# Moving attention's output ahead of DeltaNet's chain in a hybrid decoder trunk

## The chip, the core and the metric

The kernel runs on one core of a Trainium2 chip. The metric is the device time of one execution in microseconds (us), the median over runs. The engines are TensorE (PE, matrix products), VectorE (DVE), ScalarE (ACT, table functions and copies), GpSimd (POOL) and SyncE (SP, which issues the loads). Each takes its own instructions strictly in the order in which they stand, and waits at one until the data or the buffer that it needs is there.

## The reference

A trunk of two layers over 272 tokens (16 learned ones and 256) of width 1024. Each layer is

```
h = h + 0.5 * swiglu(rmsnorm(h))          # ffn1
h = h + mixer(rmsnorm(h))
h = h + 0.5 * swiglu(rmsnorm(h))          # ffn2
```

The mixer projects once to the inputs of three groups of heads and joins their outputs:

```
sb_q, sb_k, sb_v, dn_qkv, dn_z, dn_b, dn_a, s5_u = split(h @ w_in)
o_sb = rmsnorm(stick_breaking_attention(q, k, v))
qkv  = silu(causal_conv(dn_qkv))                     # q, k, v: 2 blocks of 128 columns each
o_dn = rmsnorm(chunk_gated_delta_rule(l2norm(q), l2norm(k), v, g, beta)) * silu(dn_z)
y    = gelu(s5_states_out);  o_s5 = rmsnorm(y * sigmoid(y @ w_glu + b))
return concat(o_sb, o_dn, o_s5) @ w_out
```

In the delta rule v enters only as `v * beta`. silu(x) is x·sigmoid(x), which equals 0.5·x·(tanh(x/2)+1).

## The kernel before, in words

Activations are held transposed, 128 features by 272 tokens a block. Every projection is made of three products for each pair of blocks (`mm3`, lines 139 to 143): high part by high part (L141), the activations' low part (L142), the weights' low part (L143). The weights come by DMA in pieces of 128x1024; ACT rounds a piece to its high part (`wh`, L133), and DVE or POOL subtracts to get the low part (`wl`, L136). A piece has 24 products, so a "unit" of one 128-column block is 24 products.

`mixer` works through a list of steps by hand, `MIX`. Its letters: `C0` to `C5` are the projections and causal convolutions of DeltaNet's q, k, v (two blocks each), `Q K V Z` other projections, `U`, `p`, `t`, `y` the S5 group's inputs, projections, states and outputs (`y`: products `pY`, then GELU on ACT), `g` the gates, `i` one step of the inversion of DeltaNet's triangular matrices (products `px` and `py` with copies by ACT and DVE between them), `a` one step of attention (scores, weights, and last two outputs, one for each half), `l` the silu of DeltaNet's q and v, `v` the transposed values of attention (`pvs`), `r` one step of DeltaNet's chain over its chunks, `x` one step of the S5 group's gate (`pglu`), `n` the switch of ACT's table back to Ln and Exp, `m` the S5 group's norm, `S` the part of the output projection that needs the S5 group alone, `o` DeltaNet's norm and output. The parts of the output projection that need all groups (`Y`) come after the list. The list only sets in which order the code emits its steps; a scheduler then fixes the order within each engine, and it may move an instruction past others that don't depend on it.

Attention's output step (L1271 to 1287) is, for each half: six products `pob`, a square by ACT, two products `pnb`, then Ln and Exp on ACT, three Newton steps on DVE (L118 to 120), the scaling of the output (L1284), and the split into a high part `xh` (ACT) and a low part `xl` (DVE), where the output projection reads it.

PSUM has four tags of two buffers each: `a` (projections, gate, half of the output projection), `b` (S5 and parts of DeltaNet), `c` (attention), `d` (inversion, `pob`). The scratch tile `cv` has three buffers that the convolution's `pad`, attention's `sbr` and `sby`, `zt` and others share in turn. ACT holds one set of functions at a time: Ln with Exp, silu, or GELU with tanh. `phase` loads another, and the loads keep their place among the functions that need them.

## Time and profile before

| quantity | value |
|---|---|
| runs | 1170.92, 1174.08, 1177.52 us; median 1174.08 |
| the profiled execution | 1172.99 us, its span 1170.9 us |
| TensorE | 97% of the span busy, mean granted clock 0.983 |
| VectorE, ScalarE, GpSimd | 73%, 53%, 17% |
| projections and the two ffn downs (L141 to L143) | 6 groups of products, 1840 or 528 instructions each |

The mixer of the first layer lies at about 230 to 406 us of the span, that of the second at 811 to 984. In the view of windows a PEclk of 1.00 is 2.4 GHz and 0.50 is 1.2 GHz; a window between them holds both levels. In the waits, `A <- B` means that A stood still until B was done.

### The profile page before, as it was taken

Reading aid. Unit: us, or ns where it says so; the run is one execution under the profiler, and the core shown is the slowest. Engines: PE = TensorE matmul, PEld = TensorE weight load, DVE = VectorE, ACT = ScalarE, POOL = GpSimd, SP = SyncE. Lnnn points to the kernel's source line nnn. Section 1 sums busy time; section 2 is a strip of 40 time slices with the busy share of each in tenths; the row PEclk is TensorE's granted clock in tenths of the full one; section 3 lists DMA queues with packets and bytes.
Section 4 is the critical chain, followed back from the end, with each engine's and each line's share of the span. In section 5 each row is a group of like instructions: output and inputs, shape, how many; then the busy total and the mean of one; then the engine's idle time right before and its main releaser. Section 6 shows DMA issues by size and latency. Waiting matters only on the chain.

```text
span 1170.9 us, 23748 instructions
## 1 busy us (share of the span) xinstructions
PE 1140.0 (97%) x9544; PEld 1091.7 (93%) x9544; DVE 858.5 (73%) x1609; ACT 620.5 (53%) x993; POOL 194.0 (17%) x242
## 2 busy tenths in 40 slices
PE   8999999999998999999999999999999989999997
PEld 7999999998896999999999999999988969999985
DVE  7999986599656965565569998756995678666544
ACT  6455465464663654444454555645545737545533
POOL 6312101113310111110202111011141001111100
PEclk9999999999998999999999999999999979999998
DMA  5655544542221455555565565455332216556663
GB/s 186 183 174 174 169 149 151 166 127 60 87 73 55 146 172 173 176 180 163 184 180 168 167 193 163 137 179 156 107 91 74 85 43 198 181 181 189 191 196 109
DMA packets 196858, 173.74 MB, mean 148 GB/s; under 512 B 21300, under 2 KB 193004, under 8 KB 196748
## 3 DMA queue, kind: packets, MB, share of 16 engines
q1 hardware_dynamic: 196732, 172.22, 48.6%
q8 instruction: 75, 1.23, 0.4%
q14 instruction: 35, 0.29, 0.1%
q10 hardware_dynamic: 16, 0.00, 0.0%
HBM read 171.15 MB, written 1.05 MB: 147 GB/s over the span
## 4 chain that ended last, share of the span: by engine, by line
PE 83%; DVE 10%; POOL 2%; ACT 2%; issue 2%; DMA 1%; SPq 0%; ACTq 0%; DVEq 0%; POOLq 0%
PE proj L143 17%; PE proj L142 17%; PE proj L141 17%; PE pd L143 5%; PE pd L142 5%; PE pd L141 5%; PE pd L490 5%; DVE wl L136 2%; PE pY L847 1%; POOL TT L1010 1%; PE pm L780 1%; POOL t L1009 1%; PE pob L1275 1%; PE pY L845 1%; DVE s5z L836 1%
## 5 line engine op out<-in xcount | busy, mean ns | idle before, releaser
L141 PE MATMUL proj<-xh,wh 128*128 128x272 f32 (+1 forms) x1840 | 524.8, 291 | 1.5 <-DVE sy L1424 1.5
L142 PE MATMUL proj<-xl,wh 128*128 128x272 f32 (+1 forms) x1840 | 521.9, 290 | 0.3 <-DVE xl L1222 0.3
L143 PE MATMUL proj<-xh,wl 128*128 128x272 f32 (+1 forms) x1840 | 493.4, 291 | 1.5 <-DVE wl L136 1.2
L133 ACT ACTIVATE wh<-raw 128x1024 fp32r<-128x1024 f32 (+1 forms) x324 | 338.2, 1044 | 291.5 <-PE proj L142 102.2
L136 DVE TENSOR_TENSOR wl<-raw,wh 128x1024 fp32r<-128x1024 f32 (+1 forms) x312 | 378.7, 1214 | 146.2 <-PE pd L143 60.5
L141 PEld LDWEIGHTS proj<-xh,wh 128*128 128x128 f32 x1840 | 348.8, 190 | 4.3 <-DVE sy L1424 2.6
L142 PEld LDWEIGHTS proj<-xl,wh 128*128 128x128 f32 x1840 | 348.3, 189 | 2.4 <-DVE xl L1222 0.5
L143 PEld LDWEIGHTS proj<-xh,wl 128*128 128x128 f32 x1840 | 331.4, 189 | 3.9 <-DVE wl L136 2.9
L432 POOL TENSOR_TENSOR hl<-h,hh 128x272 fp32r<-128x272 f32 (+1 forms) x88 | 80.8, 921 | 452.4 <-ACT hh L431 451.5
L141 PE MATMUL pd<-hh,wh 128*128 128x272 f32 x528 | 149.8, 289 | 0.0
L142 PE MATMUL pd<-hl,wh 128*128 128x272 f32 x528 | 149.5, 288 | 0.0
L143 PE MATMUL pd<-hh,wl 128*128 128x272 f32 x528 | 141.1, 289 | 0.2
L141 PEld LDWEIGHTS pd<-hh,wh 128*128 128x128 f32 x528 | 99.3, 188 | 0.2
L142 PEld LDWEIGHTS pd<-hl,wh 128*128 128x128 f32 x528 | 99.4, 188 | 0.1
L143 PEld LDWEIGHTS pd<-hh,wl 128*128 128x128 f32 x528 | 95.2, 189 | 1.0 <-DVE wl L136 0.9
L104 ACT ACTIVATE g<-g 128x272 f32<-128x272 f32 (+2 forms) x92 | 37.7, 415 | 68.8 <-DVE g L426 68.7
L431 ACT ACTIVATE hh<-h 128x272 fp32r<-128x272 f32 (+1 forms) x88 | 36.3, 419 | 50.7 <-DVE h L430 50.6
L430 DVE TENSOR_TENSOR h<-proj,g 128x272 f32<-128x272 f32 (+1 forms) x88 | 37.8, 434 | 32.3 <-PE proj L143 20.6
L426 DVE TENSOR_TENSOR g<-proj,R 128x272 f32<-128x272 f32 (+1 forms) x88 | 37.5, 431 | 18.3 <-PE proj L143 18.1
L428 DVE TENSOR_TENSOR g<-g,R 128x272 f32<-128x272 f32 (+1 forms) x88 | 37.8, 434 | 12.5 <-ACT g L104 12.2
L136 POOL TENSOR_TENSOR wl<-raw,wh 128x1024 fp32r<-128x1024 f32 x12 | 29.4, 2452 | 97.0 <-PE proj L143 31.9
L373 POOL TENSOR_TENSOR acc<-acc,sq 128x272 f32<-128x272 f32 (+1 forms) x20 | 23.1, 1153 | 91.9 <-ACT sq L367 91.3
(490 smaller groups left out, 1295.4 us busy)
## 6 DMA issues: line engine op xcount, KB each, us to landing
raw<-in_ffn_w_gate_dram SPq DMA_DIRECT2D x88, 512.0 KB, 3.6
raw<-in_ffn_w_up_dram SPq DMA_DIRECT2D x88, 512.0 KB, 3.7
raw<-in_ffn_w_down_dram SPq DMA_DIRECT2D x70, 512.0 KB, 3.5
raw<-in_w_in_dram SPq DMA_DIRECT2D x36, 512.0 KB, 4.3
raw<-in_ffn_w_down_dram SPq DMA_DIRECT2D x24, 384.0 KB, 3.0
raw<-in_w_out_dram SPq DMA_DIRECT2D x16, 512.0 KB, 3.4
raw<-in_s_w_glu_dram SPq DMA_DIRECT2D x4, 512.0 KB, 4.7
xin<-in_x_dram SPq DMA_DIRECT2D x4, 256.0 KB, 6.1
```

The costliest lines, as they stand in the source:

```text
L104: i = self.nc.scalar.activation(out, in_, func, **k)
L133: nc.scalar.activation(h[:, :n], r[:, :n], AF.Copy)
L136: e.tensor_tensor(l[:, :n], r[:, :n], f32(h[:, :n]), op=ALU.subtract)
L141: mm(p, wh, xh, start=first, stop=False)
L142: mm(p, wh, xl, start=False, stop=False)
L143: mm(p, wl, xh, start=False, stop=last)
L426: V.tensor_tensor(g1, pg[j][:, :N], R, op=ALU.mult)
L428: V.tensor_tensor(g1, g1, R, op=ALU.mult)
L430: V.tensor_tensor(h, pu[j][:, :N], g1, op=ALU.mult)
L431: nc.scalar.activation(hh[:, f, :N], h, AF.Copy)
L432: G.tensor_tensor(hl[:, f, :N], h, f32(hh[:, f, :N]), op=ALU.subtract)
L490: PE.matmul(pd[i][e], x[:, f, ts], w[:, 0, e * 512:e * 512 + 512], start=f == 0 and w is h and x is hh, stop=f == NF - 1 and w is lo)
```

## The change

The list is written anew. Attention's two output steps leave the end (they stood as `a` among the last `r` steps) and come before the table switch `l`; their result is written into q's place in SBUF (`q[:, b, :]`) instead of a scratch buffer, and a new step `w` (`sb_split`) makes its high and low part later, behind the second `x`. The transposed values `v` come before that, and so do `V0`, `V1`. The projections of DeltaNet's v, `C4` and `C5`, move from before `l` to behind `y0` and `y1`. Their silu no longer is among those of `l` but is made of a tanh: `twice_silu` gives (tanh(x/2)+1)·x, twice the silu, as `do_z` already did, and the half is put into beta (`beh`, one new small DVE instruction in `dn_gates`), which multiplies v later. `ON_POOL` names by their number the pieces whose low part POOL makes; the numbers stay, the pieces behind them change with the list.

```diff
@@ -39,8 +39,8 @@
-MIX = "C2 C3 U0 g U1 g g U2 g g g U3 g Q0 p0 p1 Q1 t0 p2 p3 K0 i t1 K1 a a t2 C0 a a i C1 i t3 a a i C4 i a a i C5 l i " \
-      "y0 V0 i y1 V1 i y2 Z0 y3 Z1 v r r r r x r r x r n a r r r r a m S4 S6 o S0 S2"
+MIX = "C2 C3 U0 g U1 g g U2 g g g U3 g i Q0 p0 p1 Q1 t0 p2 p3 K0 i t1 K1 i a a t2 V0 a i a C0 i a a t3 V1 i a a v i C1 a i a l " \
+      "r y0 C4 r i y1 C5 y2 r Z0 y3 r Z1 r x r x w r r n r r r m S4 S6 o S0 S2"
 ON_POOL = (5, 7, 10, 15, 20, 25)
 NBUF = (3, 2, 3)
 LO_POOL = 5
@@ -909,7 +909,9 @@
         V.tensor_copy(bet[:, 8:9], pg[:, 16:17])
         V.tensor_tensor(b8(x), pgv[:, :, 1, :], b8(dtb), op=ALU.add)
         V.tensor_tensor(x[:, 8:9], pg[:, 17:18], dtb[:, 8:9], op=ALU.add)
-        self.bet = bet
+
+        self.beh = tl([P, 9], "beh")
+        V.tensor_scalar(self.beh, bet, 0.5, None, op0=ALU.mult)
         yield
         self.phase(SET_LNEXP)
         V.scalar_tensor_tensor(g, x, -1.0, x, op0=ALU.mult, op1=ALU.min)
@@ -1087,7 +1089,7 @@
         V, G, A, PE = nc.vector, nc.gpsimd, nc.scalar, nc.tensor
         psum = lambda nm: self.psum("d", nm)
         tl, hsl, kn, TTf = self.dn_tile, self.hsl, self.kn, self.TTf
-        bet, eg, egl, el, beg = self.bet, self.eg, self.egl, self.el, self.beg
+        beh, eg, egl, el, beg = self.beh, self.eg, self.egl, self.el, self.beg
         quad = [slice(32 * q, 32 * q + 32) for q in range(4)]
         unit = lambda c, h: 4 * (h % 2) + 2 * c + h // 2
@@ -1115,7 +1117,7 @@
                 PE.transpose(pv[:, 256 + b * P:256 + b * P + P], kn[:, b, c * P:c * P + P], self.ident)
             v, k = tl([P, 4, 64], "vb", 2), tl([P, 4, 64], "kg", 2)
             pvv = pv.rearrange("p (h d) -> p h d", d=64)
-            V.tensor_tensor(v, pvv[:, 0:4], bc(bet[:, 4 * c:4 * c + 4], 2, 64), op=ALU.mult)
+            V.tensor_tensor(v, pvv[:, 0:4], bc(beh[:, 4 * c:4 * c + 4], 2, 64), op=ALU.mult)
             V.tensor_tensor(k, pvv[:, 4:8], bc(egl[:, 4 * c:4 * c + 4], 2, 64), op=ALU.mult)
             vb.append(v)
             kg.append(k)
@@ -1123,7 +1125,7 @@
         for h in range(4):
             PE.matmul(pv[32 * h:32 * h + 32, 0:64], qkv[hsl(h), 4 + h // 2, 256:288], self.ident[hsl(h), hsl(h)], start=True, stop=True)
         vbt = tl([P, 64], "vbt")
-        V.tensor_scalar(vbt, pv[:, 0:64], bet[:, 8:9], None, op0=ALU.mult)
+        V.tensor_scalar(vbt, pv[:, 0:64], beh[:, 8:9], None, op0=ALU.mult)
         yield
         qf = qkv.rearrange("p b t -> p (b t)")
@@ -1275,17 +1277,21 @@
                 PE.matmul(p[:, 0:272], vt[0][:, h, :], W[h][:, 0:272], start=True, stop=False)
                 PE.matmul(p[:, 128:272], vt[1][:, h, :], W[h][:, 272:416], start=False, stop=False)
                 PE.matmul(p[:, 256:272], vt[2][:16, h, :], W[h][:16, 416:432], start=False, stop=True)
-            r, y = self.cv("sbr")[:, :T], self.cv("sby")[:, :T]
+            r, y = self.cv("sbr")[:, :T], q[:, b, :]
             A.activation(r, po[:, :T], AF.Square)
             pn = psum("pnb")
             PE.matmul(pn[:, :T], self.bd64, r, start=True, stop=True)
             self.rsqrt(r, pn[:, :T], scale=1.0 / 64, bias=self.eps)
             self.newton(r, pn[:, :T], y, 64, EPS)
             V.scalar_tensor_tensor(y, po[:, :T], self.sbg[:, l], r, op0=ALU.mult, op1=ALU.mult)
-            h = self.xh[:, slot + b, :]
-            A.activation(h, y, AF.Copy)
-            V.tensor_tensor(self.xl[:, slot + b, :], y, f32(h), op=ALU.subtract)
-
+
+        def split():
+            for b in range(2):
+                h = self.xh[:, slot + b, :]
+                A.activation(h, q[:, b, :], AF.Copy)
+                V.tensor_tensor(self.xl[:, slot + b, :], q[:, b, :], f32(h), op=ALU.subtract)
+
+        self.sb_split = split
         for f, x in ((scores, 0), (scores, 1), (weights, 0), (scores, 2), (weights, 1), (scores, 3),
                      (weights, 2), (weights, 3), (outputs, 0), (outputs, 1)):
             f(x)
@@ -1357,6 +1363,12 @@
             ba = tmp.tile([8, TP], F32, name="ba")
             G.memset(ba[:, T:], 0.0)
+            def twice_silu(x):
+
+                t = self.cv("ts")[:, :T]
+                self.act(t, x, AF.Tanh, scale=0.5)
+                V.scalar_tensor_tensor(x, t, 1.0, x, op0=ALU.add, op1=ALU.mult)
+
             def conv(b):
                 src = w_in[:, 768 + b * P:768 + b * P + P]
                 if b == 2:
@@ -1372,6 +1384,8 @@
                     V.scalar_tensor_tensor(y, pad[:, k:k + T], self.cw[:, l, k, b:b + 1], y, op0=ALU.mult, op1=ALU.add)
                 if b in (2, 3):
                     self.act(y, y, AF.Silu)
+                elif b > 3:
+                    twice_silu(y)
             u = tmp.tile([P, 4, T], F32, name="s5u")
             zr = tmp.tile([P, 2, T], F32, name="pz")
@@ -1387,16 +1401,12 @@
                 V.scalar_tensor_tensor(dst[:, b, :], p[:, :T], 0.125 if c0 == 0 else 1.0, R, op0=ALU.mult, op1=ALU.mult)
             def do_z(b):
-
                 proj(1536, zr, b)
-                t = self.cv("zt")[:, :T]
-                self.act(t, zr[:, b, :], AF.Tanh, scale=0.5)
-                V.scalar_tensor_tensor(zr[:, b, :], t, 1.0, zr[:, b, :], op0=ALU.add, op1=ALU.mult)
+                twice_silu(zr[:, b, :])
             def silu():
                 self.phase(SET_SILU)
-                for b in (0, 4):
-                    self.act(qkv[:, b:b + 2, :T], qkv[:, b:b + 2, :T], AF.Silu)
+                self.act(qkv[:, 0:2, :T], qkv[:, 0:2, :T], AF.Silu)
                 self.phase(SET_GELU)
             def norms():
@@ -1429,7 +1439,7 @@
                           a=self.sb(l, q, k, v, 0), x=self.glu(l, u))
             steps = dict(C=conv, U=s5_in, Q=lambda b: proj(0, q, b), K=lambda b: proj(256, k, b), V=lambda b: proj(512, v, b),
                          Z=do_z, p=lambda r: self.s5_inputs(u, r), t=self.s5_states, y=lambda r: self.s5_outputs(u, r),
-                         l=silu, v=lambda: self.sb_values(), n=norms, S=lambda d0: w_out_part("S", d0, "ab"[d0 // 2 % 2]),
+                         l=silu, v=lambda: self.sb_values(), w=lambda: self.sb_split(), n=norms, S=lambda d0: w_out_part("S", d0, "ab"[d0 // 2 % 2]),
                          o=lambda: (self.dn_norm(), self.dn_out(zr, self.dng[:, l], 2)),
                          m=lambda: self.rms(self.acc, 4 * 512, 0, self.R5, "b"))
             for x in MIX.split():
```

Three places show what the order within the engines becomes.

TensorE, from the inversion's third product (`px`, L1040 before and L1042 after) on. Before:

```order
L141 MATMUL proj<-xh,wh 128x272
L1040 MATMUL px_4060<-T_4047,LT 32x32 x16
L142 MATMUL proj<-xl,wh 128x272
...
L143 MATMUL proj<-xh,wl 128x272
L845 MATMUL pY<-s5U,M_591 128x68
L847 MATMUL pY<-s5z_3458,W_589 128x68
...
L1053 MATMUL py_4127<-kb,TT_4048 32x32 x8
L1056 MATMUL py_4127<-TT_4048,kb 32x32 x16
L847 MATMUL pY<-s5z_3458,W_590 128x68
```

After:

```order
L143 MATMUL proj<-xh,wl 128x272
L1042 MATMUL px_4042<-T_3975,LT 32x32 x16
L1055 MATMUL py_4087<-kb,TT_3976 32x32 x8
L1058 MATMUL py_4087<-TT_3976,kb 32x32 x16
L1277 MATMUL pob<-W_587 64x272
...
L1075 MATMUL px_4181<-T_3975,LT 64x32 x8
L1277 MATMUL pob<-W_587 64x272
...
L1080 MATMUL py_4302<-TTf,X_4170 64x64 x8
L1283 MATMUL pnb<-sbr,bd_385 128x272
L141 MATMUL proj<-xh,wh 128x272
```

Fourteen projection products and five of S5's outputs stood between `px` and `py`; none does now. The inversion's and attention's small products stand in one row, and the projection behind the second `pnb` is Z's first.

VectorE, around the convolution of C4 and the decays `E` of DeltaNet. Before, where `E` is made:

```order
L1318 SCALAR_TENSOR_TENSOR s5u_3079<-th_4466,s5u_3079 128x272
L1324 SCALAR_TENSOR_TENSOR xl_95<-s5u_3079,prm_361,xh_94 128x272 x3
L883 TENSOR_TENSOR E_3299<-pl_4422,E_3299 128x512
L1330 TENSOR_TENSOR rs_4467<-rs_4467,gsq_4586 128x272
L887 TENSOR_TENSOR Et_3359<-plt_4428,Et_3359 128x32
```

After, from attention's second output on:

```order
L1286 SCALAR_TENSOR_TENSOR pq_3081<-pob_4191,prm_361,sbr_4198 128x272
L1381 TENSOR_TENSOR pad_4274<-proj_4243,R_3061 128x272
L1384 SCALAR_TENSOR_TENSOR qkv_3075<-pad_4274,prm_361,qkv_3075 128x272 x3
L1370 SCALAR_TENSOR_TENSOR qkv_3075<-ts_4281,qkv_3075 128x272
L1381 TENSOR_TENSOR pad_4361<-proj_4330,R_3061 128x272
L1384 SCALAR_TENSOR_TENSOR qkv_3075<-pad_4361,prm_361,qkv_3075 128x272 x3
L1105 TENSOR_SCALAR eq_4224<-pn_4211 128x9
...
L1370 SCALAR_TENSOR_TENSOR pz_3080<-ts_4445,pz_3080 128x272
L1292 TENSOR_TENSOR xl_95<-pq_3081,xh_94 128x272 x2
L883 TENSOR_TENSOR E_3301<-pl_4290,E_3301 128x512
L887 TENSOR_TENSOR Et_3361<-plt_4296,Et_3361 128x32
```

`pq` is q's place. C4's `pad`, which empties the PSUM buffer that Z's first projection writes, stands behind attention's second output; `eq` stands behind C5's convolution, and the second `E` behind the two splits of attention's output.

TensorE at the end of DeltaNet's chain. Before:

```order
L1161 MATMUL pS<-qkv,E 128x64 x4
L1281 MATMUL pnb<-sbr,bd_385 128x272
L1176 MATMUL pkt<-qkv,kn 32x64
...
L1177 MATMUL pkt<-qkv 32x64
L1184 MATMUL pvt_4646<-rt_4642,TTt 32x64 x4
L1188 MATMUL pvt_4646<-vnt,Et 32x64 x4
L1275 MATMUL pob<-W_587 64x272
```

After:

```order
L1179 MATMUL pkt<-qkv 32x64
L141 MATMUL proj<-xh,wh 128x272
L142 MATMUL proj<-xl,wh 128x272
...
L141 MATMUL proj<-xh,wh 128x272
L1186 MATMUL pvt_4671<-rt_4667,TTt 32x64 x4
L141 MATMUL proj<-xh,wh 128x272
...
L143 MATMUL proj<-xh,wl 128x272
L1190 MATMUL pvt_4671<-vnt,Et 32x64 x4
```

The S5 group's part of the output projection now stands among `pkt`, `pvt` and `pvt`, where attention's products were.

## Rows read from the trace of the kernel before

**Rows 1.** the page: busy us of each engine, share of the span, instructions

```profile
PE 1140.0 (97%) x9544; PEld 1091.7 (93%) x9544; DVE 858.5 (73%) x1609; ACT 620.5 (53%) x993; POOL 194.0 (17%) x242
```

**Rows 2.** windows: start and end, us, busy (instructions) by engine, PEclk, DMA share, GB/s

```profile
core 0: us, PE busy (x) PEld busy (x) DVE busy (x) ACT busy (x) POOL busy (x), PEclk, DMA share, GB/s
259.00:267.00 8.00, 8.00 (x40) 6.90 (x39) 6.19 (x15) 0.77 (x2) 0.11 (x1) 0.57 0.22 62
297.00:365.00 68.00, 65.49 (x884) 60.69 (x883) 40.37 (x74) 40.88 (x77) 10.55 (x15) 1.00 0.28 86
369.00:370.00 1.00, 0.74 (x2) 0.52 (x3) 0.63 (x3) 0.76 (x2) 0.00 (x0) 0.52 0.06 16
370.00:380.00 10.00, 8.52 (x33) 5.79 (x32) 6.37 (x20) 2.82 (x8) 0.29 (x1) 0.54 0.00 0
860.00:864.00 4.00, 4.00 (x22) 3.76 (x22) 4.00 (x7) 2.49 (x5) 0.28 (x1) 0.57 0.08 22
946.00:960.00 14.00, 11.48 (x62) 7.88 (x56) 9.75 (x29) 3.81 (x10) 0.29 (x1) 0.52 0.00 0
```

**Rows 3.** TensorE's waits, 297 to 390 us: line, releaser, us in total, times, longest

```profile
PE pkt L1176 <- DVE qkv L1170: 1.3, 1, 1.3
PE proj L141 <- DVE sy L1424: 1.1, 2, 0.7
PE px L1021 <- DVE T L1014: 1.0, 1, 1.0
...
PE pob L1275 <- DVE sby L1284: 0.3, 1, 0.3
```

**Rows 4.** the same view, second layer, 876 to 970 us

```profile
PE px L1021 <- DVE T L1014: 0.5, 1, 0.5
...
PE proj L141 <- DVE sy L1424: 0.4, 1, 0.4
```

**Rows 5.** timeline of TensorE: start, us, engine, line, output<-inputs, count

```profile
312.06 0.29 PE L142 MATMUL proj<-xl,wh 128*128 128x272 f32 x1
312.18 0.29 PE L143 MATMUL proj<-xh,wl 128*128 128x272 f32 x1
...
318.74 0.69 PE L1040 MATMUL px<-T,LT 32*32 32x32 f32 x32
...
364.88 0.68 PE L1281 MATMUL pnb<-sbr,bd 128*128 128x272 f32 x2
```

**Rows 6.** timeline of ScalarE, same columns

```profile
309.97 1.28 ACT L94 ACT_TABLE_LOAD   x1
311.26 1.21 ACT L104 ACTIVATE qkv<-qkv 128x544 f32<-128x544 f32 x2
...
314.07 1.59 ACT L104 ACTIVATE s5u<-pY 32x272 f32<-32x272 f32 x4
...
319.48 0.36 ACT L1044 COPY kb<-px 32x256 f32<-32x256 f32 x1 [0.22 <-PE px L1040]
...
321.35 1.06 ACT L133 ACTIVATE wh<-raw 128x1024 fp32r<-128x1024 f32 x1 [1.50 <-PE proj L142]
...
365.60 0.49 ACT L104 ACTIVATE sbr<-pnb,eps 128x272 f32<-128x272 f32 x1 [1.53 <-PE pnb L1281]
366.11 0.43 ACT L104 ACTIVATE sbr<-sbr 128x272 f32<-128x272 f32 x1
...
369.24 0.43 ACT L1286 ACTIVATE xh<-sby 128x272 fp32r<-128x272 f32 x1 [0.67 <-DVE sby L1284]
```

**Rows 7.** timeline of VectorE, same columns

```profile
328.63 0.43 DVE L1074 COPY X<-px 64x256 f32<-64x256 f32 x1 [3.82 <-PE px L1073]
...
348.63 0.68 DVE L883 TENSOR_TENSOR E<-pl,E 128x512 f32<-128x512 f32 x1
...
367.76 0.43 DVE L119 SCALAR_TENSOR_TENSOR sby<-sby,sbr 128x272 f32<-128x272 f32 x1
...
369.70 0.44 DVE L1287 TENSOR_TENSOR xl<-sby,xh 128x272 fp32r<-128x272 f32 x1 [0.37 <-ACT xh L1286]
```


## The prediction

> **What bounds the kernel now.** The page comes first: TensorE (PE) is busy 97% of the span [rows 1], so the time is PE's work plus the places where PE stands or runs at the low clock. Then the view of windows over the first layer's mixer [rows 2]. In the long middle stretch, 297 to 365, PE is busy 65.49 of 68.00 us at a granted clock of 1.00. In the tail behind it, attention's and DeltaNet's last products, it is busy 0.74 of 1.00 and 8.52 of 10.00 us, at clocks of 0.52 and 0.54. Two further stretches run low, 259 to 267 and 860 to 864 (0.57 both), in which PE is busy throughout with small products. With the level at 0.5 or 1.0, the low part of a window is twice its length times what is missing to 1.00: 8.0 x 2 x 0.43 = 6.9 us, 3.4 us, in the first tail 1.0 + 9.2 = 10.2 us, in the second (946 to 960) 13.4 us. Last PE's waits [rows 3, 4]: in the first layer seven of them, from `pkt` (1.3) to `pob` (0.3), belong to the tail and come to 4.8 us; in the second the same ones repeat, but `proj` stands at 0.4 where the first has 1.1, and `pob` has none: 3.8. The other long waits of the middle are `px` with 1.0 and 0.5.
>
> So the tail is what can be won: 8.6 us of waits, and the low clock. At full clock its busy part would take half: 10.2 x 9.26/11.00 / 2 = 4.3 us, and 13.4 x 11.48/14.00 / 2 = 5.5 us. That makes 18.4 us in all. The price is what the middle, now almost dense, has to give.
>
> **The change, part by part.** The order shown above is that of the built kernel; each term is a place where PE comes early, priced by the chain that it then waits for. The number of PE's products is the same, and no load is added; SP's queue keeps its length, and only the order of its pieces follows the list.
>
> *beh.* One DVE instruction on nine columns a layer, in the gates, where PE is fed by other work: nothing. Two 1.2 us silus of 544 columns [rows 6] become one, and two tanh with a DVE step each take its place; ACT is at 53% and DVE at 73%: nothing directly. ON_POOL gives POOL other pieces; each low part is asked for a unit later, so nothing, and one DVE subtraction more or less if that cover is gone.
>
> *First inversion product.* Between attention's last scores and it stood twenty products of projections; now there are eleven. A product takes 0.126 us (312.06 to 312.18) [rows 5], so PE comes 9 x 0.126 = 1.1 us earlier, and by what else is moved behind it 0 to 0.5 more. What it waits for (`T`, a 1.0 us wait before, [rows 3]) doesn't move: **+1.4 us** a layer, 1.1 to 1.6.
>
> *Second `py`.* Behind `px` (0.69 us, [rows 5]) come a copy by ACT, 0.36 at 319.48, and one by DVE, 0.43. Nineteen products covered them; now nothing stands between. From the start of `px` at 318.74 to ACT's copy at 319.48 is 0.74, then 0.36 + 0.04 + 0.43 and a handover of some 0.15: 1.7, less the 0.6 that PE is busy, is 1.1. If ACT first finishes a rounding of weights (1.06, [rows 6]) it is 1.5. **+1.3.**
>
> *Second `pob`.* It takes the PSUM buffer that DVE's copy X has to empty, 0.43 [rows 7] and handovers: **+0.6**, 0.5 to 0.7.
>
> *Z's first product.* It needs C4's PSUM buffer, which DVE's `pad` empties, and `pad` stands on DVE behind attention's second output. From the second `pnb` on (0.68, [rows 5]): Ln 0.49, Exp 0.43 [rows 6], three root steps of 0.43 [rows 7], a scaling of about 0.5, `pad` about 0.43, together 3.1, with six handovers of 0.04 to 0.15 some 3.6; and 0.2 more because PE is free before `pnb` has landed. Nothing of PE stands between: **+3.7**, 3.5 to 3.9. What is queued behind the waiting product is all of the rest, S5's outputs and DeltaNet's start. In before the same chain ran beside the tail, and cost there what rows 3 show.
>
> *`pl` and `eq`.* DVE makes `eq` behind C5's convolution; PE comes by some 0.7 too early: **+0.7**, 0 to 1.5 (three convolution steps).
>
> *S5's second output.* It needs the buffer that the second `E` empties, and `E` stands on DVE behind the two splits of attention's output, which wait for ACT's rounding, queued behind one of weights that waits for Z1's last product. After that come xh 0.43 twice [rows 6], xl 0.44, E 0.68 [rows 7], handovers 0.3, less 0.1 of overlap: 2.2 from Z1's last product. **+2.0**, 1.4 to 2.2.
>
> *DeltaNet's chain and the gate.* The gate's products no longer stand beside the chain's first half, and two GELU groups of 1.59 us [rows 6] come ahead of products of PE. All of it hidden gives 0; both groups bare, with a split (0.43 + 0.44) and a copy, give 4.5. **+3.0**, nearer to the upper end, as the order has only S5's and DeltaNet's own small products in between.
>
> *The new tail.* The chain `pkt`, `pvt`, `pvt` waited 4.8 in all [rows 3]. Now 24 products of S4 stand among them, 3.0 us of cover, which would leave 1.8. But the table load (1.28, [rows 6]) now stands on ACT ahead of the copy that the last `pvt` waits for, and S4's products wait themselves for the split of S5's gated output. With no cover and the load on top it is 6.1. **+3.8**, about the middle.
>
> Sum of a layer: 1.4 + 1.3 + 0.6 + 3.7 + 0.7 + 2.0 + 3.0 + 3.8 = 16.5 us; in the second layer 0.5 more, as its first `pnb` follows its `pob` at once. Two layers: +33.5. Against it stand 8.6 and 9.8 us: **+15.1 us** if the clock falls nowhere new.
>
> *The clock.* Among the first waits of the old tail, with small products and gaps before it, the level was down (369 to 370, 0.52) [rows 2]; what now stands before Z is the same mixture (`px`, `py`, `pob`, `pnb`, a wait of 3.7). So I take one fall a layer. The four seen last 3.4, 6.9, 10.2 and 13.4 us, on average 8.5; at the tails' busy share of 0.83 one costs 8.5 x 0.83 / 2 = 3.5, less 0.6 because the wait of `pl` is covered when the products ahead of it take longer: +2.9 each, **+5.8**. None gives 0, falls like those of the tails (10.2 and 13.4) with later waits uncovered give 9.8.
>
> The profiled execution took 1173.0 us (span 1170.9). 1173.0 + 15.1 + 5.8 = 1193.9; the median of the runs is 1.1 above it: **1195 us**.
>
> A rule beside a row. ACT's table load at 309.97 takes 1.28 us, and the next function starts at 311.26, at once [rows 6]. Behind attention's last Exp now come load, silu (0.6), load and two squares (about 0.4 each), 4.0 us, before `pn`; from that Exp to `pn` PE waits and works on Z for about 5.1 us, so they are hidden. The Trainium skill, "ScalarE: Activation LUTs", section "What ACT_TABLE_LOAD costs", adds a drain of about 1.38 us to each switch of 1.28. By that, two switches would take 2.8 us more, 1.7 of them bare, and the sum would be 3.4 us higher, 1198; the row shows no such drain, so I leave it out.
>
> **The rivals.**
> *The clock stays up.* The middle's waits are short ones, and in before waits of 1.4 and 1.0 us [rows 3] in the stretch 297 to 365 left it at 1.00 [rows 2]; against it, a wait of 3.7 is longer than any there. 1173.0 + 15.1 + 1.1 = 1189.
> *More or longer falls.* Two a layer, one in the middle and one in the new tail, whose waits lie close together as in before; another 5.8, or 9.8 in place of 5.8 with the terms at their upper ends: 1201 to 1211, say 1205.
> *The other side: the other engines are ahead of PE.* My terms treat each wait as bare. The stretch 297 to 365 interleaves the same chains and loses 2.5 us in 68 [rows 2]. If the new middle and tail, some 83 us, lose at that rate, it is 3.1 us a layer against 7.3 now (2.5 and 4.8), so 8.4 less for both, and the low clock's 9.8 come back too: 1174.1 - 18.2 = 1156. It decides at Z's first product: 3.6 us of other work for PE between the second `pnb` and it hide that chain. The order shows none there, which speaks against it.
> *The moves cancel.* All terms at their lower ends (1.1, 1.1, 0.5, 3.5, 0, 1.4, 0, 1.8 = 9.4 a layer) make 18.8 against 18.4: 1174.5, no change.
> *It doesn't do what it says.* The words put C4 and C5 among S5's outputs; the built order has their products ahead of the inversion's third product, only their convolution behind. That is in the sum already.
>
> **How the numbers follow.** Forecast 1195: 0.45. Clock stays up, 1189: 0.18. More or longer falls, 1205: 0.20. Other side, 1156: 0.10. No change, 1174: 0.07. A measurement of this kernel tells about 0.5% (5.9 us) from no change. The first three are slower by over that, together 0.83; same 0.07; faster 0.10. The range must leave out 0.2: the other side and most of no change below, little above the upper ends: 1178 to 1211.
>
> **What would show it.** In the changed profile: a wait of `proj` L141 for `pad` (L1381) of about 3.7 us in each layer, the longest; `py` for `kb` with 1.1 to 1.5; `pY` for `E` with about 2; `pvt` for `rt` and `vnt`, and no `pob`, `pnb` or `po` wait at the end; the granted clock at 1.00 where the old tail was, and a lower one behind Z's wait. I am wrong if that wait is under 1 us, if the low clock appears nowhere (1189), or if the table load is followed by idle time of ACT.

## The result and the profile after

The changed kernel took 1205.99 us in the median (1200.73 to 1211.74), against 1175.80 for the kernel before in the same comparison: a ratio of 1.0278, with an interval of 1.0232 to 1.0324. It is slower by some 30 us. The prediction was 1195, with a range of 1178 to 1211.

The profiled execution took 1201.4 us. The page of after, its span, its engines and the granted clock in 40 slices:

```profile
span 1199.3 us, 23763 instructions
PE 1154.1 (96%) x9544; PEld 1100.9 (92%) x9544; DVE 858.9 (72%) x1615; ACT 620.9 (52%) x995; POOL 190.1 (16%) x242
...
PEclk9999999998889999999999999999996899999998
```

Beside [rows 1] this splits the loss in two. TensorE (PE) is busy 1154.1 us where it was 1140.0: 14.1 more, with the same 9544 products. It stands 45.2 us (1199.3 - 1154.1) where it stood 30.9: 14.3 more. Together they are the 28.4 us between the two spans. Most of the busy part is the clock. Its mean was 0.983 before and is 0.972 now, so the time at the low level (1.2 GHz) is 2 x 1170.9 x 0.017 = 39.8 us and 2 x 1199.3 x 0.028 = 67.2 us. PE was busy in 29.7 us of it before and in 52.4 now, by windows of 2 us. Half of this difference, 11.4 us, is what the products lost by running at the low level; the other 2.7 us of the busy part are not traced.

Where the clock was low, in the view of windows of after (columns as in [rows 2]: start and end, length, busy time with instructions of PE, PEld, DVE, ACT, POOL, then the granted clock, the DMA share and GB/s):

```profile
275.00:289.00 14.00, 12.79 (x69) 10.87 (x67) 13.97 (x24) 5.91 (x10) 3.65 (x6) 0.76 0.28 78
297.00:322.00 25.00, 23.15 (x510) 19.95 (x509) 13.68 (x24) 11.34 (x22) 3.88 (x6) 1.00 0.29 87
322.00:336.00 14.00, 10.52 (x47) 8.03 (x48) 5.94 (x13) 6.29 (x11) 0.10 (x1) 0.51 0.01 1
366.00:372.00 6.00, 5.14 (x51) 4.63 (x52) 5.87 (x11) 4.62 (x9) 2.11 (x1) 1.00 0.29 89
372.00:382.00 10.00, 8.34 (x58) 6.89 (x57) 7.33 (x18) 7.56 (x14) 0.00 (x0) 0.83 0.24 66
910.00:934.00 24.00, 19.06 (x101) 14.72 (x99) 7.36 (x17) 8.74 (x16) 0.20 (x2) 0.52 0.01 2
934.00:944.00 10.00, 10.00 (x60) 9.62 (x60) 5.31 (x11) 4.11 (x9) 0.00 (x0) 0.66 0.03 5
970.00:980.00 10.00, 7.89 (x65) 6.47 (x64) 7.18 (x15) 8.82 (x13) 0.00 (x0) 0.83 0.26 85
```

The old tails are nearly clean: 3.4 us at the low level in 372 to 382 and in 970 to 980, where [rows 2] had 10.2 and 13.4. But the middle, which ran at 1.00 throughout before (297 to 365 in the first layer, 876 to 946 in the second), now holds 13.7 us (322 to 336), and in the second layer 23.0 + 6.8 us (910 to 944). A third place, 275 to 289, holds 6.7 us, as much as 259 to 267 held before.

Where PE stood in the first layer's mixer, 225 to 440 us:

```profile
PE proj L141 <- DVE pad L1381: 3.5, 1, 3.5
PE proj L141 <- DVE sy L1434: 1.8, 1, 1.8
PE proj L143 <- DVE wl L136: 1.4, 3, 0.6
PE pz L1253 <- DVE pk L1401: 1.2, 1, 1.2
...
PE pvt L1186 <- DVE rt L1181: 0.7, 1, 0.7
PE pglu L141 <- ACT xh L1310: 0.6, 1, 0.6
...
PE pvn L1155 <- DVE vb L1120: 0.5, 1, 0.5
```

And three of the places foretold, in PE's timeline of after (start, length, line, output<-inputs; in brackets the idle time before and its releaser):

```profile
315.38 0.59 PE L1055 MATMUL py<-kb,TT 32*32 32x32 f32 x13 [0.83 <-ACT kb L1046]
...
321.94 0.91 PE L1277 MATMUL pob<-W 128*64 128x272 f32 x2 [0.52 <-DVE X L1076]
...
327.38 1.27 PE L1283 MATMUL pnb<-sbr,bd 128*128 128x272 f32 x2
332.13 0.60 PE L141 MATMUL proj<-xh,wh 128*128 128x272 f32 x1 [3.48 <-DVE pad L1381]
```

Z's first product (L141, at 332.13) stands 3.48 us for `pad` behind the second `pnb`; the second `py` 0.83 for ACT's copy; the second `pob` 0.52 for the copy X. In the second layer the three are 3.5, 0.8 and 0.5 again. These are the chains that [rows 5 to 7] were read for. The fall of the clock starts ahead of the longest of them: in the first layer at 322, behind the waits of 0.83 and 0.52, and in the second in 909 to 910, behind `py`'s alone (0.8 and 0.2) and some 15 us before `pad`'s wait begins:

```profile
909.00:910.00 1.00, 1.00 (x6) 0.60 (x5) 0.42 (x1) 0.23 (x1) 0.00 (x0) 0.67 1.02 357
```

### The profile page after: what moved, and what is told of

It is laid out like the page before. It is cut to its first block, busy times and chain, and to the rows that moved or that the text cites. A ratio compares the mean times of both kernels' runs of the same rounds, so it can differ in the third digit from the quotient of the medians.

```text
span 1199.3 us, 23763 instructions
## 1 busy us (share of the span) xinstructions
PE 1154.1 (96%) x9544; PEld 1100.9 (92%) x9544; DVE 858.9 (72%) x1615; ACT 620.9 (52%) x995; POOL 190.1 (16%) x242
## 4 chain that ended last, share of the span: by engine, by line
PE 79%; DVE 12%; ACT 3%; issue 2%; DMA 2%; POOL 2%; ACTq 0%; SPq 0%; DVEq 0%; POOLq 0%
PE proj L143 16%; PE proj L141 16%; PE proj L142 16%; PE pd L143 5%; PE pd L142 5%; PE pd L141 5%; PE pd L490 5%; DVE wl L136 3%; PE pY L847 1%; DVE xl L362 1%; DVE xT L1436 1%; DVE s5U L809 1%; PE pm L780 1%; PE pY L845 1%; PE pob L1277 1%
## 5 line engine op out<-in xcount | busy, mean ns | idle before, releaser
L141 PE MATMUL proj<-xh,wh 128*128 128x272 f32 (+1 forms) x1840 | 527.2, 292 | 10.8 <-DVE pad L1381 7.0
L141 PEld LDWEIGHTS proj<-xh,wh 128*128 128x128 f32 x1840 | 350.2, 191 | 16.3 <-DVE pad L1381 8.5
L141 PE MATMUL pd<-hh,wh 128*128 128x272 f32 x528 | 149.6, 288 | 0.0
L141 PEld LDWEIGHTS pd<-hh,wh 128*128 128x128 f32 x528 | 99.2, 188 | 0.2
```

The lines of the kernel that those rows point to most:

```text
L141: mm(p, wh, xh, start=first, stop=False)
```

## Experiments

Each run is compared with the kernel before on the same chip; a ratio over 1 is slower. "Low" is time at the low level, added up from windows of 2 us. A diff of a list shows only the part of `MIX` that differs, and `...` marks lines of an edit that are left out. A trace is one execution of four or more; where it is far from the median, the text says so. The trace has two records for each of the small products of this kernel (`px`, `py`, `pob`, `pnb`, `pY`), so x4 are two of them.

**The silu alone.** The list of before, with the silu of DeltaNet's v from a tanh, behind the switch to GELU's table:

```diff
+        V.tensor_scalar(self.beh, bet, 0.5, None, op0=ALU.mult)
...
-                for b in (0, 4):
-                    self.act(qkv[:, b:b + 2, :T], qkv[:, b:b + 2, :T], AF.Silu)
+                self.act(qkv[:, 0:2, :T], qkv[:, 0:2, :T], AF.Silu)
                 self.phase(SET_GELU)
+                for b in (4, 5):
+                    twice_silu(qkv[:, b, :T])
```

> The list of the kernel before, with only the silu of DeltaNet's v made of a tanh behind the switch to GELU's table, and beta halved. Theory A (the loss comes from TensorE standing, and falling to the low clock, in the stretch in which the inversion's and attention's small products now stand alone): one silu of 0.6 us on ScalarE against two tanh of 0.43 and two DVE steps of 0.43, all beside other work, so the time of before within 0.3%, 1173 to 1179 us. Theory B (the loss comes from the new silu or from the rest of the new list): 5 us or more above before, 1181 or more.

Measured: 1173.67 us, ratio 0.999 (0.9971 to 1.0009). No difference: the arithmetic of the change costs nothing, and the loss lies in the list and what goes with it (q's place, the later split).

**The wait for pad, taken away by the list.** C4 put ahead of attention's last steps:

```diff
-v i C1 a i a l r y0 C4 r i y1 C5 y2 r Z0
+v i C1 C4 a i a l r y0 r i y1 C5 y2 r Z0
```

> The changed kernel with C4 put ahead of attention's last two steps in the list; Z's products then stand between px, py, pob and the first pnb, and the norm's pn stands right behind the second pnb. Theory A: py's wait of 0.8 and Z's of 3.5 go, but pn now waits for what is queued on ScalarE behind the second pnb (Ln 0.5, Exp 0.4, load 1.3, silu 0.7, load 1.3, squares 0.8: 4.9 us, 4.5 of them bare), so idle time stays within 1 us a layer; the stretch of small products stays from the second px of this group on, so the clock still falls, later and for a shorter time: 1195 to 1206 us. Rival (the wait for pad is the loss itself, once it is gone its time is gone): 2 x 4.3 less, with the low clock behind it, 1190 us or less.

Measured: 1242.76 us, ratio 1.058 (1.0547 to 1.0612), the slowest of all and outside both ranges. The wait of Z is gone, and `pn` waits in its place, as theory A had it, but longer:

```profile
PE pn L1101 <- ACT sq L1099: 7.0, 1, 7.0
```

```profile
326.00:394.00 68.00, 57.25 (x290) 52.30 (x290) 17.31 (x43) 26.81 (x53) 4.27 (x3) 0.52 0.05 16
```

The second fence is the view of windows in the first layer: for 68 us, from the inversion's last products to those of the gate, the clock stands at 0.52. But this run does not move C4's products alone. C4's tanh now stands among attention's logarithms and exponentials, and ACT loads a table ten times more than in the changed kernel (1005 instructions against 995). Two of these loads stand between the second `pnb` and `pn`:

```profile
336.19 1.28 ACT L104 ACT_TABLE_LOAD   x1
337.48 0.49 ACT L104 ACTIVATE sbr<-pnb,eps 128x272 f32<-128x272 f32 x1
337.99 1.28 ACT L104 ACT_TABLE_LOAD   x1
```

So theory A had the wait of `pn`, and these two loads make most of the 2.5 us by which it exceeds the 4.5 expected. The low stretch holds the small products of the inversion, of S5's outputs and of DeltaNet, but towards its end, from 378 on, also the gate's products of 128x272. Why the level stays down for all of it is not shown.

**Attention's outputs back at the end.** The new list otherwise:

```diff
-v i C1 a i a l r y0 C4 r i y1 C5 y2 r Z0 y3 r Z1 r x r x w r r n r r r m S4 S6 o S0 S2
+v i C1 i l r y0 C4 r i y1 C5 y2 r Z0 y3 r Z1 r x r x r r n a r a r w r m S4 S6 o S0 S2
```

> The changed kernel with attention's two output steps taken out of the middle and put back among the last steps, behind the switch to Ln and Exp; all else of the new list stays (values early, C4 and C5 late, tanh, q's place, the split behind them). The outputs' products now stand among the gate's and the output projection's. Theory A: the bare stretch is gone in the middle, and in the tail products of projections stand between them, so no waits for pad and X, low clock for under 10 us a layer: 1160 to 1178 us. Theory B (the rest of the list costs the time): 1190 us or more.

Measured: 1202.20 us, ratio 1.0232 (1.0192 to 1.0272). Theory A as it stood is wrong: the outputs are out of the middle, and nearly all of the loss is still there. Its windows over S5's outputs in the two layers:

```profile
318.00:342.00 24.00, 24.00 (x204) 22.00 (x203) 9.27 (x21) 6.08 (x14) 0.10 (x1) 0.64 0.11 35
...
912.00:948.00 36.00, 36.00 (x257) 34.24 (x253) 10.23 (x24) 8.54 (x20) 0.10 (x1) 0.57 0.10 30
```

PE is busy 24.00 of 24.00 and 36.00 of 36.00 us, and the clock is 0.64 and 0.57. The view of waits has none in these stretches, so the level falls without one. The stretches are not small products only: up to 941, 15 products of projections stand among those of the second. That left two questions: whether waits matter to the level at all, and which part of the list makes this stretch.

**The wait for pad, filled.** In `outputs`, behind the second `pnb` of the changed kernel, products that nothing reads:

```diff
             PE.matmul(pn[:, :T], self.bd64, r, start=True, stop=True)
+            if b == 1:
+                fill = psum("fill")
+                for j in range(28):
+                    PE.matmul(fill[:, :T], self.xh[:, 2, :P], self.xh[:, 3, :], start=j == 0, stop=j == 27)
```

> The changed kernel with 28 products of 128x272 (about 0.126 us each at the full clock, 3.5 us; 0.23 at the low one, 6.4 us) behind the second pnb, into a PSUM tile that nothing reads, so that TensorE works through the wait for pad. Theory A (the level falls in the small products ahead of the wait, at 322 in the trace of after): it still falls at the same place, and the dense products bring it back some 2 to 4 us sooner; about what the extra products cost at the low clock beyond the wait: 1198 to 1208 us. Rival C (the 3.5 us wait is what brings the level down or holds it down): no low clock in this place in either layer, some 18 us a layer at the low level become full, 1190 to 1196 us.

Measured: 1198.08 us, ratio 1.0223 (1.0177 to 1.0268), in the range of theory A. By the median that is 8 us under the changed kernel, though 7 us of products were added (56 x 0.126); the intervals of the two overlap. The profiled execution is the fastest of the four (1195.39 us, at a mean clock of 0.980; the others had 0.971 to 0.975, inside the 0.965 to 0.977 of the changed kernel). In it the low level nearly goes from this place, as rival C had it:

```profile
322.00:336.00 14.00, 13.48 (x127) 10.27 (x121) 5.03 (x12) 5.26 (x11) 0.00 (x0) 0.88 0.12 39
904.00:934.00 30.00, 28.65 (x370) 25.39 (x369) 15.86 (x33) 14.78 (x28) 1.58 (x6) 1.00 0.17 54
```

0.88 in 322 to 336 (3.4 us low), 1.00 in 904 to 934. But this is not the work of the fill, which comes too late for it:

```profile
331.00:332.00 1.00, 1.00 (x12) 0.68 (x11) 0.00 (x0) 0.39 (x1) 0.00 (x0) 0.90 0.00 0
332.94 3.90 PE L1287 MATMUL fill<-xh 128*128 128x272 f32 x28
904.00:921.00 17.00, 15.65 (x264) 12.89 (x262) 8.03 (x15) 5.73 (x11) 1.38 (x4) 1.00 0.30 95
```

In the first layer the level falls at the second `pob`, as in the changed kernel, and is back in 331 to 332, before the fill starts at 332.94. In the second layer the changed kernel falls at the first `pob`, in 909 to 910; here TensorE comes through the same `px`, `py` and `pob` at 1.00 and reaches the fill only at 920.89. So the two executions differ ahead of anything that the edit adds. The fill can have kept the level up through the wait, no more, and whether the wait of 3.5 us matters to the level is not shown.

**C5 held back.** The scheduler had moved C5's products ahead of the inversion's third product. Here an order between instructions of TensorE holds them back (`at` names, for a block `k` of the unit, the product behind which it has to stand):

```diff
+                if k in at:
+                    g = lambda x: getattr(x, "ins", x)
+                    self.order(g(i), g(self.anchor[at[k]]))
...
-                    p, = self.unit(src, P)
+                    p, = self.unit(src, P, at={0: "px2", 3: "pob0", 5: "pob1"} if b == 5 else {})
```

> The changed kernel with C5's 24 products held back on TensorE: the first nine may only stand behind px (L1042 of after), the next six behind attention's first output products, the last nine behind its second ones. Theory A, as the first four runs left it (the level falls where small products stand in a row without products of projections among them, with waits or without): py's wait of 0.8 and X's of 0.5 go, Z's of 3.5 stays within 1 us since pad still stands behind attention's second output; low clock in the middle 14 and 31 us in the two layers before, now less than half of it; 1185 to 1197 us. Rival (only TensorE's standing counts, and where the projections' products stand doesn't): 2 x 1.3 less than after, 1200 to 1206.

Measured: 1205.03 us, ratio 1.0280 (1.0227 to 1.0332). `py`'s wait is gone, Z's is down to 2.9, X's is still 0.5, and a new one has come up for the product that C5 had covered:

```profile
PE proj L141 <- DVE pad L1387: 2.9, 1, 2.9
...
PE px L1043 <- DVE T L1033: 0.9, 1, 0.9
```

The low level didn't go: in the profiled execution (1213.55 us, the longest of four) the clock was 0.71 in 322 to 330, 0.50 from 330 to 342 and 0.71 to 350. Over all four the mean clock is 0.961 to 0.980, no better than the changed kernel's 0.965 to 0.977. Twenty-four products among the small ones of this stretch did not help, and moving them opened the place that they came from. The forecast of theory A fell. The time is the rival's, but its reason isn't shown either: the waits hardly shrank in sum, so this run doesn't tell what a smaller sum of waits would give.

**V early, alone.** The kernel before with V0 and V1 where the changed kernel has them:

```diff
-K1 a a t2 C0 a a i C1 i t3 a a i C4 i a a i C5 l i y0 V0 i y1 V1 i y2 Z0
+K1 a a t2 V0 C0 a a i C1 i t3 V1 a a i C4 i a a i C5 l i y0 i y1 i y2 Z0
```

> The kernel before with one edit in its list: V0 and V1 stand where the changed kernel has them, ahead of the inversion's later steps and S5's outputs, and no longer among these. Attention's outputs stay at the end, C4 and C5 ahead of l, silu as it was. 48 products of projections leave the stretch of S5's outputs; up to 12 of their small ones now stand in a row, and 22 with px and py among them. Theory A': that is what costs in the changed kernel and in the run with the outputs late; low clock in the middle of each layer, some 10 to 17 us, and waits of px and py of about 1 us: 1180 to 1192 us. Rival (moving attention's outputs, or C4 and C5, costs it): 1171 to 1178.

Measured: 1185.63 us, ratio 1.0098 (1.0074 to 1.0123), in the range of theory A'. Two windows of this run over the inversion's end and S5's outputs:

```profile
324.00:345.00 21.00, 21.00 (x145) 20.55 (x145) 5.96 (x12) 9.27 (x23) 1.80 (x1) 0.67 0.10 28
904.00:925.00 21.00, 21.00 (x224) 20.16 (x223) 5.20 (x11) 10.05 (x22) 1.18 (x3) 0.76 0.17 51
```

The kernel before ran at 1.00 all through the first of these stretches (297 to 365, [rows 2]). Here the clock is 0.67 (13.9 us low) and 0.76 (10.1 us), and PE is busy 21.00 of 21.00 us in both: no wait at all. What changed is that 48 products of projections are gone from among the small ones. In the trace of this run:

```profile
323.76 1.11 PE L1069 MATMUL px<-kb,LT 64*64 64x32 f32 x16
...
325.08 0.61 PE L847 MATMUL pY<-s5z,W 128*128 128x68 f32 x4
...
328.54 1.06 PE L847 MATMUL pY<-s5z,W 128*128 128x68 f32 x4
```

At 325.08 four records of `pY` take 0.61 us, at 328.54 they take 1.06. From 323.76 on only `px` and `pY` stand between. The one longer wait of this part, `px` with 1.5, lies ahead of 300, and from there to the fall at 328 PE is busy without a break. By windows of 2 us each fall lasts 13.6 us in all; the second ends behind its window. So V's place costs about 12 us in the old list, and it is the clock: PE is busy 1153.2 us in this run, 13.2 more than before, and half of the low time in which it was busy is 13.6 more.

**C4 and C5 late, alone.** The kernel before with the tanh and with C4, C5 among S5's outputs:

```diff
-C1 i t3 a a i C4 i a a i C5 l i y0 V0 i y1 V1 i y2 Z0
+C1 i t3 a a i i a a i l i y0 V0 C4 i y1 V1 C5 i y2 Z0
```

> The kernel before with the silu of DeltaNet's v by tanh and one edit in its list: C4 and C5 stand behind V0 and V1 among S5's outputs, and no longer ahead of l. V, values and attention's outputs stay where they were. Products of projections then stand among the inversion's last products and S5's outputs, up to 24 in a row, and at most eight of S5's small ones. Theory A' (it is where the projections stand, not which of the changed steps is late): no low clock in the middle, waits in the first part of it within 2 us of before: 1172 to 1180 us. Rival (late C4 and C5 are a cost of their own, through their convolution on VectorE): 1183 or more.

Measured: 1174.95 us, ratio 1.0008 (0.9986 to 1.0031): no difference. The same windows as above read

```profile
324.00:345.00 21.00, 21.00 (x195) 20.21 (x194) 11.15 (x19) 13.43 (x30) 4.17 (x2) 1.00 0.25 76
904.00:925.00 21.00, 21.00 (x195) 20.16 (x194) 11.02 (x19) 13.45 (x29) 2.35 (x1) 1.00 0.24 77
```

with PE as busy as there, and the clock at 1.00 (the trace is the fastest of ten, 1170.43 us). This is what the change's words promise (DeltaNet's v among S5's outputs), and it is neutral. It costs nothing where projections remain between.

**V late, the rest of the new list with the outputs at the end.** The diff is against the list of the run with the outputs late; the values `v` move with V:

```diff
-t2 V0 a i a C0 i a a t3 V1 i a a v i C1 i l r y0 C4 r i y1 C5 y2 r Z0
+t2 a i a C0 i a a t3 i a a i C1 i l r y0 V0 C4 r i y1 V1 C5 v y2 r Z0
```

> The run with the outputs late, with V0 and V1 put back among S5's outputs and the values v behind them: of the new list the late C4 and C5, the earlier r and the interleaved tail stay. Theory A': most of the 28 us over before goes, 1172 to 1186 us, with low clock under 10 us in each middle. Rival (C4 and C5 late, or the earlier steps of DeltaNet's chain, cost it by themselves): 1195 to 1205.

Measured: 1195.57 us, ratio 1.0186 (1.0153 to 1.0218), in the rival's range: by the median about 7 us better than with V early, with intervals that overlap, not the 16 to 30 that theory A' asked for. In the trace, the longest of the four (1200.27 us), low clock remains in the middles, in stretches that add up to 27 us in the first layer (300 to 364) and 27 in the second (894 to 958). With V's place mended, the order built from this list still shows 11 and 13 `pY` in a row around the last `py`. Whether it is the earlier steps of DeltaNet's chain (`r`) or something else in the list that draws the projections away from there was not tried.

**Fill among S5's outputs, V early.** Four products that nothing reads behind each of two groups of `pY` in every output:

```diff
+            if b % 2 == 0:
...
+                f = self.psum("c", "fill")
+                for j in range(4):
+                    i = PE.matmul(f[:, :T], self.xh[:, 6, :P], self.xh[:, 7, :], start=j == 0, stop=j == 3)
...
```

> The run with V0 and V1 early, with products that nothing reads among S5's outputs: two groups of four of 128x272 for each of the four outputs, 32 in a layer, 4.0 us at the full clock. TensorE was busy 21.00 of 21.00 us there, at a granted clock of 0.67 in the first layer and 0.76 in the second, so each of these products is added work. Theory A' (the small products in a row bring the level down): the low clock of 13.6 us in each middle goes; it is worth 6.8 us, so the time falls by about 3 us a layer although work is added: 1176 to 1183 us. Rival (the level falls for another reason): the work is added, at a low clock for part of it: 1192 to 1200 us.

Measured: 1187.04 us, ratio 1.0114 (1.0072 to 1.0155), between the two forecasts. The trace is the longest of the four (1193.10 us; the others 1185.42 to 1187.14). In it the low level stays:

```profile
324.00:345.00 21.00, 21.00 (x194) 20.44 (x191) 3.61 (x7) 6.56 (x17) 0.58 (x1) 0.76 0.05 15
904.00:925.00 21.00, 21.00 (x269) 20.21 (x260) 5.95 (x12) 8.55 (x18) 1.76 (x4) 0.82 0.09 27
```

The first layer has 10.2 us low in this place, where the run without fill had 13.6; the second has 13.6 in both, of which the window shows 7.6. Eight us of work were added and the median rose by 1.4, which the intervals of the two runs can't tell from none. This one is not decided: the four mean clocks are 0.974 to 0.978 against 0.970 to 0.977, so the fill may give back part of its price, and how much dense work such a stretch needs is left open.

**The tail of before, filled.** No other change:

```diff
+    def fill(self, n, after, rhs=3):
...
+        t = self.psum("c", "fill")
+        for j in range(n):
+            i = self.nc.tensor.matmul(t[:, :T], self.xh[:, 6, :P], self.xh[:, 7, :], start=j == 0, stop=j == n - 1)
...
+        pin = self.fill(10, last)
```

`fill` puts `n` products into a tile that nothing reads: 10 ahead of `pkt`, 5 and 3 ahead of the two `pvt`, 4 and 6 around the second `pnb`.

> The kernel before, with products of 128x272 that nothing reads put into the waits of its tail: 10 ahead of pkt (1.3 us wait), 5 and 3 ahead of the two pvt (0.7, 0.3), 4 ahead of the second pnb (0.5), 6 behind it (po, 0.6), 28 in each layer, 3.5 us at the full clock against 3.4 us of waits. Nothing else is changed. Theory C (TensorE's standing between small products is what brings the level down): the low clock of the tails (10.2 and 13.6 us, worth 4.3 and 5.5) goes or falls below 4 us a layer at no cost: 1163 to 1170 us. Theory A (the small products bring it down, standing or not): the low clock stays, and the fill costs up to 3 us a layer in it: 1174 to 1182 us.

Measured: 1168.21 us, ratio 0.9961 (0.9947 to 0.9975). It is the one version that is faster than both kernels clear of noise, though it does 56 products more. Its page and the two tails:

```profile
PE 1138.4 (98%) x9600; PEld 1093.2 (94%) x9600; DVE 854.7 (73%) x1609; ACT 620.5 (53%) x993; POOL 196.4 (17%) x242
```

```profile
365.00:380.00 15.00, 13.65 (x119) 11.46 (x118) 11.63 (x34) 5.46 (x13) 0.44 (x1) 1.00 0.00 1
944.00:960.00 16.00, 14.13 (x112) 11.96 (x111) 12.94 (x34) 6.14 (x13) 2.74 (x2) 1.00 0.10 34
```

```profile
364.47 1.63 PE L1088 MATMUL fill<-xh 128*128 128x272 f32 x10
366.12 0.32 PE L1186 MATMUL pkt<-qkv,kn 64*32 64x64 f32 x7
...
368.68 0.67 PE L1296 MATMUL pob<-W 128*64 128x272 f32 x2
```

Against [rows 2]: where before had 0.52 to 0.54 the clock is 1.00 in both tails. The ten products at 364.47 end where `pkt` starts, at 366.12, which waited 1.3 us before [rows 3]. The six attention products begin at 368.68 with 0.67 us a pair, as at the full clock. Theory C's forecast came and theory A's fell. But the fill does two things at once: it takes most of the gaps away (of these waits `pvt` keeps 0.2), and it puts products of 128x272 among the small ones. Which of the two keeps the level up, this run can't tell. PE is busy 1.6 us less than before, with more to do.

**The tail of before, filled by real products.** Two lists that bring `m`, S4, S6 and S0 among the last `a` and `r`; the first:

```diff
-y0 V0 i y1 V1 i y2 Z0 y3 Z1 v r r r r x r r x r n a r r r r a m S4 S6 o S0 S2
+y0 V0 i y1 V1 v i y2 Z0 y3 Z1 r r r r x r r x n r a m S4 S6 a r r S0 r r S2 o
```

> The kernel before, silu and all else as it was, with only its list rewritten from y0 on: values earlier, and m, S4, S6, S0 among the last a and r, so that products of the output projection stand between attention's output products, pnb, pkt and pvt in the tail; the middle keeps C4, C5, V and Z among S5's outputs. Theory A: the middle stays at full clock, the tail loses its waits (4.8 and 3.8 us before) and its low clock (10.2 and 13.6 us, worth 4.3 and 5.5): up to 18 us under before, 1157 to 1168. Rival (what is taken from the tail comes back as waits elsewhere, as in the changed kernel): 1172 or more.

> As the run with the filled tail, in another order: values where they were, m, S4 and S6 ahead of the last a and r, S0 between the last two r, so that 38 products stand ahead of attention's first output products and 13 to 9 between the later ones, but five only between the second output's products and its pnb, and po and pnb stand together. Theory A: the gain is smaller than with an even spread, 1160 to 1172; rival as there: 1172 or more.

Measured: 1183.63 us, ratio 1.0087 (1.0064 to 1.0111), and 1181.78 us, ratio 1.0071 (1.0043 to 1.0099). Both are slower; theory A fell in both. In the first the tail's low clock shrank (3.4 us in the first layer, 3.4 and 6.8 in the second; 31 us in the whole program, 41 before), but waits took its place:

```profile
PE proj L141 <- DVE sy L1424: 3.1, 2, 1.9
...
PE proj L141 <- ACT xh L1221: 1.2, 1, 1.2
```

The output projection's parts need PSUM buffers that VectorE empties (`sy`, L1424), and it does so behind the chain's own small steps; 3.1 us for `sy` alone, 1.2 for the high part of DeltaNet's output at the end. In the second, `pvt` waits 2.3, and the low clock stays (13.6 us from 376, 17.0 from 956). Real products are no free filling: each unit holds a buffer and brings evictions with it.

## Why the prediction came out as it did

The direction was right, and the sum for the profiled execution to within 8 us (1193.9 forecast, 1201.4 measured; the median came 11 us above the forecast). That it came so near is luck: two of its parts were wrong by more than that, in opposite directions.

**Standing: +24.9 us net forecast, +14.3 measured.** Term by term:

- Z's first product: 3.7 forecast, 3.5 in both layers; second `py` 1.3, 0.8; second `pob` 0.6, 0.5. These three chains, read step by step from [rows 5 to 7], held within 0.5 us.
- The second layer's 0.5 more, for the first `pnb`: there, with 0.5; beside it `px` waits 0.5 for X, which was not foretold.
- The first inversion product: 1.4 more a layer forecast. In the first layer `px` doesn't wait at all now (1.0 before), and 1.2 us appear earlier, where attention's scores (`pz` L1253) wait for k's projection. In the second layer `px` and this `pz` have 1.2 each (0.5 each before). In sum 1.6 more, where 2.8 were forecast. The prediction also passes over attention's other `pz`, which waits for `W`: 1.4 in both layers before, 0.5 and 1.4 now.
- `pl` for `eq`: 0.7 forecast, none measured.
- S5's second output for `E`: 2.0 forecast, none measured. This step failed for a reason that can be read. I had the split of attention's output wait for Z1's last product. It writes blocks 0 and 1 of `xh`, though, and a unit goes through the blocks in order, so they are free after six of its products. In the trace of after ACT's split runs while Z1 is still going on (DVE's `E` behind it, and last the eviction of Z1, waiting for its last product):

```profile
343.59 0.73 ACT L1291 ACTIVATE xh<-pq 128x272 fp32r<-128x272 f32 x2
```

```profile
345.27 0.69 DVE L883 TENSOR_TENSOR E<-pl,E 128x512 f32<-128x512 f32 x1 [0.19 <-PE pl L882]
...
346.93 0.44 DVE L1401 SCALAR_TENSOR_TENSOR pz<-proj,R 128x272 f32<-128x272 f32 x1 [0.87 <-PE proj L143]
```

- DeltaNet's chain and the gate: 3.0 forecast, 0.5 + 0.6 measured (`pvn`, `pglu`). The value near the upper end was the wrong choice; S5's small products covered the GELUs.
- The tail: 3.8 forecast. The waits of S4's products and of the first `pvt` in the first layer, 366 to 382, come to 0.86 + 1.66 = 2.5 us by the windows above; in the second layer those of S4's products come to 2.8.
- Not foretold: 1.8 us for `sy` further on in the first layer, and 1.4 and 1.6 us for the low parts of ffn2's first weights, for which VectorE comes late. Before had none of the latter in 390 to 600.

**The clock: -4.0 us net forecast (9.8 back from the tails, 5.8 for new falls), +11.4 measured.** That the tails' low clock would go was nearly right: 3.4 us a layer are left in them, and half of the time that PE was busy at it there, 9.8 us before, is some 3 now, so nearly 7 came back. The term for new falls was mis-sized, and it is what failed most: 8.5 us of low clock a layer forecast; measured, 13.7 in the first (322 to 336; the 6.7 of 275 to 289 stand in place of those of 259 to 267) and 29.8 in the second (910 to 944). By the same half they cost 18 us, where 5.8 was forecast. The rival "more or longer falls", 1205, has the time, by longer falls in the middle and short ones in the new tail. I sized the fall by the mean length of falls that had ended among other products. What decides the length is not shown: both layers have the same list, and the level came back at 336 in the first, among Z's products, and fell again at 937 in the second, among `pY` and `pl`. And I put the fall down to Z's wait: the run with V early shows that no wait is needed, and the fall in after starts ahead of Z's wait in both layers.

A rule of the Trainium skill is weighed by these runs. "TensorE: Matmul & The Clock Gate", section "HAM oscillation — how this bites in real kernels", ties the fall of the clock to gaps in which the engine is idle. The run with V early does not fit it (0.67 with 21.00 of 21.00 us busy). The fill of the tails (0.52 to 1.00) doesn't decide it, since it filled short gaps, of 1.3 us at most, with dense products. For this kernel a stretch of mostly small products is one way to the low level; that idle gaps alone are another, no run here shows.

The other rule, the drain behind a table load ("ScalarE: Activation LUTs", "What ACT_TABLE_LOAD costs"), again doesn't show. ACT's timeline of after, behind attention's last Exp:

```profile
329.65 1.28 ACT L94 ACT_TABLE_LOAD   x1
330.95 0.66 ACT L104 ACTIVATE qkv<-qkv 128x544 f32<-128x544 f32 x1
```

The load takes 1.28 us and the next function starts at once; the second load, at 331.62, reads the same, and `pn` waited for neither.

What the change cost, as far as the runs settle it: nothing for the tanh (ratio 0.999) and nothing for C4 and C5 late by themselves (1.0008); about 12 us for V early in the old list, by the clock alone. The list with V early and the outputs late is 27 us over before, the full change 30, and putting V back in the former gave some 7, so the costs don't simply add. How the last 15 to 18 us divide between the earlier chain of DeltaNet, the outputs' place and both together is open: with the outputs late they are low clock and waits at other places, with the outputs in the middle they are Z's 7 us of waits and the low clock around them.

## What to carry to other kernels

Count the dense products between the small ones, not only the waits: a unit moved to an earlier place leaves a stretch that may be fully busy and still run at half speed. Before a step is moved forward, ask which products it takes along and what then stands alone where they were. And where a chain of small steps can't be filled with real work, products that nothing reads, sized to the waits, can be cheaper than the low clock, as in the filled tail (56 products more, 0.4% less time). In a stretch that was already busy throughout they did not pay (1187.04 against 1185.63 us).

## What the runs showed of the hardware

The low level doesn't need a wait. With V early TensorE was busy without a break from 300 us on, and at 328 the granted clock fell to 0.50 (0.67 over 324 to 345, at 21.00 of 21.00 us). With the outputs late it was 0.57 at 36.00 of 36.00 us (912 to 948), among products of 128x68 and smaller with short rows of projections between them. "Busy" is what the profile's records cover, and their ends are modelled: no gap was seen, which does not mean that the array was full.

The level differs between executions of one program, and the time with it: the four runs of the changed kernel took 1200.73, 1201.4, 1210.59 and 1211.74 us at mean clocks of 0.977, 0.972, 0.967 and 0.965. The spread of 11 us is about what these clocks give (an estimate: 0.012 x 1205 = 14 us). So four executions, and one trace, tell little about a difference of a few us in a kernel with such falls. With the tails filled the eight runs lie within 3.8 us, at 0.993 to 0.998.
